# The gate's column sums spread over four due times, and later

## The chip, the cores and the metric

One core of one Trainium2 chip runs the kernel. The metric is the device time of one execution in microseconds (us). Three runs of the kernel before took 1739.5, 1739.6 and 1740.47 us; the median is 1739.6. One more execution was taken with the hardware profiler: 1735.66 us, of which the instructions span 1733.9 us.

## The reference

All data are float32, with 256 tokens and a width of 4096.

```
mod = SiLU(c) @ w_ada + b_ada              # -> shift, scale, gate (4096 each)
h   = RMSNorm(x) * (1 + scale) + shift
P   = h @ w_in                             # 4096 -> 14336 columns, in 7 groups of 2048
y_A = B * conv3(C * xa) * SiLU(z_A)        # causal depthwise conv over tokens
y_B = SiLU(LN(conv31(v * sigmoid(g)))) * SiLU(z_B)
x   = x + gate * ([y_A, y_B] @ w_out)      # 4096 -> 4096
out = RMSNorm(x) * final_g
```

The vector `gate` is needed only at the end, when the tiles of the output projection are finished.

## The kernel before, in words

**Matrix products.** Each f32 weight tile is loaded by SyncE's DMA queue (SP), in pieces of 256 rows by 512 columns (512 KB; a few of half that). ScalarE (ACT) rounds a piece to its high part (`w_h`, L217), VectorE (DVE) subtracts to get the low part (`w_l`, L218), and TensorE (PE) makes three products, high by high, high by low and low by high (L244 to L246). A slice of 128 rows takes 6 matmuls of 512 columns. The kernel counts its progress in these slices: `now` is the number of slices done, and is called the position here. A weight piece is mostly two slices, called a step. Positions 0 to 896 are the input projection, 896 to 1024 the first half of the output projection (tiles `pa0` to `pa7`, from the half y_A), 1024 to 1152 its second half (`pb0` to `pb7`, from y_B). Pieces are numbered in order: `w480` belongs to position 930, and `w519` to 1008.

**Buffers.** There are 4 buffers for raw pieces, 3 each for `w_h` and `w_l`, so a new piece can be rounded only when PE has ended with the piece three steps earlier. Pieces are asked for two steps ahead (`next_w`). Transposes and small reductions on PE go to a pool of two PSUM banks (`misc`), of which a new tile takes one that the program has already released.

**The modulation.** Columns of `shift`, `scale` and `gate` come from products of rows of w_ada with a broadcast SiLU(c) on DVE: one instruction (L271) for half of each of 128 columns, from a loaded row piece of 1 MB. These are called sums. There are 128 for shift and scale, and 64 for the gate (`gate0_0` to `gate31_1`), which fill the columns of `gateT`.

**Order of the work.** Everything is issued by a program written out in order. At each step `run_due` first issues what stands in `queue` with a due time at or before `now`. Then it takes from `filler`, the list of sums: a sum is issued when it is due, or ahead of that when a running estimate of DVE's and the DMA's load leaves room. The due times of the sums are interpolated along a hull of the points by which so many must be done (`need`). For all 64 gate sums one such point stands at position 1004. Four positions later `gate_store` transposes `gateT` on PE (L300), ACT copies the result four positions after that (L303) and writes it to `gate_d` in DRAM (L304). From there `load_resid` (L725 to L729) loads broadcast rows of `final_g` and of the gate, 1024 columns for two output tiles at a time, and `x` for each output tile, at positions 1026, 1042 and so on.

**Beside the products.** From about position 750 the 31-tap convolution of half B runs: ACT makes scaled copies (`pr`, L500), DVE adds them to `cv` (L503) or makes a tap by itself (L496). It goes on to position 970. Then the layer norm follows (`norm_B`, positions 972 to 1010), and at 1011 to 1025 the eight steps of `gate_B`: PE transposes 256 columns of SiLU(z_B) into a `misc` bank (`psZ0_0` to `psZ3_1`, L581), DVE multiplies `cv` by them (L584, called gated here), and both are split into `yT`. In the second half of the output projection DVE has three instructions per finished tile (L693, L696, L703).

The choice of what to take from the list of sums is this line:

```
due, mb, cost, f = filler[0]
if due > now and (max(vec, t - SLACK) + cost > t + UNIT * KD or max(load, t - SLACK) + mb / RATE > t + UNIT):
    break
```

Of the kernel before, what the change touches and what calls it, by code (L numbers as in the profile page):

```python
# [13 lines left out]
F32 = mybir.dt.float32  # L14
# [4 lines left out]
P = 128  # L19
D = 4096  # L20
S = 256
NS = S // P
KT = D // P
CT = 512
NE = 7 * 2048 // CT
NDT = D // CT
# [4 lines left out]
BLOCKS = (2, 4, 4, 4, 6, 6, 6)  # L31
# [3 lines left out]
KD = 2  # L35
# [6 lines left out]
UNIT = 1.363  # L42
FIRST = 29.0
RATE = 0.375
# [4 lines left out]
SLACK = 3.0  # L49
# [59 lines left out]
def decoder_block(ctx: ExitStack, tc: tile.TileContext, x, c, w_mod, w_gate, w_in, w_out, xt, pk, final_g, out):  # L109
    nc = tc.nc  # L110
# [11 lines left out]
    dram = ctx.enter_context(tc.tile_pool(name="dram", bufs=1, space=bass.MemoryType.DRAM))  # L122
# [3 lines left out]
    def bigt(name, shape=(P, 2, 512), dtype=F32):  # L126
        return big.tile(list(shape), dtype, tag="a", name=name)

    def misc(name, shape=(P, 512)):
        return pms.tile(list(shape), F32, tag="m", name=name)  # L130

    def pst(name):
        return pmm.tile([P, NS, CT], F32, tag="ps", name=name)
# [3 lines left out]
    ident = const.tile([P, P], F32, name="ident")  # L137
# [32 lines left out]
    end_in = sum(n for _, _, n in plan)  # L170
    start_last = sum(k1 - k0 for b, _, k0, k1 in SEGS if b < len(BLOCKS) - 1)
    conv_end = end_in + CONV_END
    plan += [(w_out[dt], k0 + k, KD) for k0 in (0, KT // 2) for dt in range(NDT) for k in range(0, KT // 2, KD)]
    loaded = []
    step = 0
    now = 0
    queue = []
    filler = []
    vec = load = 0.0

    def put(t, f, cost=0.0):
        queue.append((t, cost, f))
        queue.sort(key=lambda e: e[0])
# [5 lines left out]
    def run_due():  # L189

        nonlocal vec, load
        t = FIRST + UNIT * now
        while queue and queue[0][0] <= now:
            _, cost, f = queue.pop(0)
            vec = max(vec, t - SLACK) + cost
            f()
        while filler:
            due, mb, cost, f = filler[0]
            if due > now and (max(vec, t - SLACK) + cost > t + UNIT * KD or max(load, t - SLACK) + mb / RATE > t + UNIT):
                break  # L200
            filler.pop(0)
            vec = max(vec, t - SLACK) + cost
            load = max(load, t - SLACK) + mb / RATE
            f()
# [53 lines left out]
    gateT = const.tile([P, KT], F32, name="gateT")  # L258
# [4 lines left out]
    def ada_steps(name, srcs, bias, dst):  # L263

        at = next(part_no) % 4
        pt = pts[:, at:at + 1]

        def piece(q):
            raw = rows.tile([P, ROW], F32, tag="r", name=f"{name}_{q}")
            nc.sync.dma_start(raw, srcs[q])  # L270
            nc.vector.tensor_tensor_reduce(out=raw, in0=raw, in1=cB[:, q * ROW:(q + 1) * ROW], scale=1.0, scalar=pt if q else bias, op0=ALU.mult, op1=ALU.add, accum_out=dst if q else pt)  # L271

        return [lambda q=q: piece(q) for q in range(D // ROW)]

    def mod_steps(k):

        def scale(f):
            f()
            nc.vector.scalar_tensor_tensor(out=gscT[:, k:k + 1], in0=modT[:, 32 + k:33 + k], scalar=1.0, in1=pks[:, O_G + k:O_G + k + 1], op0=ALU.add, op1=ALU.mult)

        work = []
        for t in (1, 0):
            col = 32 * t + k
            work += ada_steps(f"mod{k}_{t}", w_mod[k, t], pks[:, O_BADA + col:O_BADA + col + 1], modT[:, col:col + 1])
        work[1] = lambda f=work[1]: scale(f)
        return work

    gate_d = dram.tile([D], F32, name="gate_d")
    gate = {}

    def gate_steps():
        return [f for k in range(KT) for f in ada_steps(f"gate{k}", w_gate[k], pks[:, O_BGATE + k:O_BGATE + k + 1], gateT[:, k:k + 1])]

    def gate_store():

        ps = misc("gate_ps", (P, P))
        row = bigt("gate_row", (P, P))

        def turn():
            nc.tensor.transpose(ps[:KT], gateT, ident)  # L300

        def store():
            nc.scalar.copy(row[:KT], ps[:KT])  # L303
            nc.scalar.dma_start(gate_d.rearrange("(k p) -> k p", p=P), row[:KT])  # L304

        turn()
        put(now + 2 * KD, store)
# [35 lines left out]
    for q in range(4):  # L343
        for s in range(NS):
            t = bigt(f"xn{q}_{s}", (P, 1024))
# [14 lines left out]
    for q in range(4):  # L360
        ps = pst(f"cps{q}")
# [7 lines left out]
    v, y, t = (tiny[:, i] for i in range(3))  # L369
# [12 lines left out]
    ps = misc("rstd_ps", (P, S))  # L382
# [12 lines left out]
    vec = load = FIRST - SLACK  # L395


    work = [f for k in range(1, KT) for f in mod_steps(k)]
    gates_due = end_in + KT // 2 * NDT - 20
    need = [(FIRST_USE[k] - H_DUE, len(work) * k // (KT - 1)) for k in range(1, KT)]  # L400
    work += gate_steps()
    need.append((gates_due, len(work)))
    hull = [(-3.0, 0)]
    while hull[-1][1] < len(work):
        t0, n0 = hull[-1]
        hull.append(max((p for p in need if p[1] > n0), key=lambda p: ((p[1] - n0) / max(p[0] - t0, 0.1), p[0])))
    for n, f in enumerate(work):
        filler.append((float(np.interp(n + 1, [d for _, d in hull], [t for t, _ in hull])), ADA_LOAD, ADA_SUM, f))
    put(gates_due + 4, gate_store)
    for ks in [[1]] + [[k, k + 1] for k in range(KD, KT, KD)]:  # L410
        for (f, cost), lead in zip(h_steps(ks), H_LEAD):
            put(FIRST_USE[ks[0]] - lead, f, cost)
# [180 lines left out]
    def seed(n):  # L593


        _, e, k0, _ = SEGS[n]
        ps = pst(f"ps{k0}_{e}")
        if k0:
            nc.scalar.copy(ps, acc[e])  # L599
        return ps  # L600
# [30 lines left out]
    ps = seed(0)  # L631
    for n, (b, e, k0, k1) in enumerate(SEGS):
        steps = _steps(k0, k1)
        for j, (k, m) in enumerate(steps):
            parts = begin_step()
            if j == max(len(steps) - 2, 0) and n + 1 < len(SEGS):
                ps_next = seed(n + 1)
            run_due()
            products(ps, act_h, parts, k, m, k == 0, k + m == k1, seeded=k0 > 0)
            advance()  # L640
        pending.append(lambda e=e, k1=k1, ps=ps: take(e, k1, ps))
        ps = ps_next
# [4 lines left out]
    for i in range(4):  # L647
        for h in range(2):
            t = end_in + NORM_AT + NORM_STEP * (19.5 + 2 * i + h)
# [20 lines left out]
    for dt in range(NDT):  # L670
        ps = pst(f"pa{dt}")
        for k in range(0, KT // 2, KD):
            parts = begin_step()
            if dt == NDT - 1 and k == KD * 4:
                ps_next = seed_b(0)
            run_due()
            products(ps, yT, parts, k, KD, k == 0, k + KD == KT // 2)
            advance()
        pending.append(lambda dt=dt, ps=ps: take_a(dt, ps))
# [7 lines left out]
    def finish_tile(dt, ps):  # L687

        o, xr = res[dt], resid[dt]
        g, fg = half(gate, dt), half(fgb, dt)  # L690

        def gated():
            nc.vector.tensor_tensor(out=o, in0=ps, in1=g, op=ALU.mult)  # L693

        def residual():
            nc.vector.tensor_tensor(out=o, in0=o, in1=xr, op=ALU.add)  # L696

        def squares():
            for s in range(NS):
                nc.scalar.activation(out=xr[:, s], in_=o[:, s], func=AF.Square, accum_out=sums[:, s, dt:dt + 1])  # L700

        def weighted():
            nc.vector.tensor_tensor(out=o, in0=o, in1=fg, op=ALU.mult)  # L703

        def ahead():
            table(AF.Sqrt)
            nc.vector.tensor_tensor(out=o, in0=o, in1=g, op=ALU.mult)
            nc.vector.tensor_tensor(out=o, in0=o, in1=xr, op=ALU.add)

        def last(s):  # L710
            t = scratch[:, s]
            nc.vector.tensor_tensor(out=t, in0=ps[s], in1=g[:, s], op=ALU.mult)
            nc.vector.tensor_tensor(out=o[:, s], in0=o[:, s], in1=t, op=ALU.add)
            nc.scalar.activation(out=t, in_=o[:, s], func=AF.Square, accum_out=sums[:, s, dt:dt + 1])
            nc.vector.tensor_tensor(out=o[:, s], in0=o[:, s], in1=fg[:, s], op=ALU.mult)

        if dt == NDT - 1:
            scratch = bigt(f"t{dt}")
            return [ahead] + [lambda s=s: last(s) for s in range(NS)]
        return [gated, residual, squares, weighted]  # L720

    def load_resid(dt):
        if dt % 2 == 0:
            t = fgb[dt // 2] = bigt(f"fg{dt // 2}", (P, 1024))
            nc.sync.dma_start(t, final_g[dt * CT:dt * CT + 1024].partition_broadcast(P))  # L725
            t = gate[dt // 2] = bigt(f"gate{dt // 2}", (P, 1024))
            nc.sync.dma_start(t, gate_d[dt * CT:dt * CT + 1024].partition_broadcast(P))
        xr = resid[dt] = bigt(f"xr{dt}")
        nc.sync.dma_start(xr, xv[:, :, dt * CT:(dt + 1) * CT])  # L729

# [8 lines left out]
    ps = ps_next  # L739
    for dt in range(NDT - 1):  # L740
# [8 lines left out]
        ps = ps_next  # L749
# [4 lines left out]
    for k in range(KT // 2, KT, KD):  # L754
        held[k] = begin_step()
        run_due()
        if k == KT // 2 + 4 * KD:
            work = finish_tile(NDT - 1, pss)
# [6 lines left out]
    for s in range(NS):  # L765
# [4 lines left out]
        v, y, t = (const.tile([P, 1], F32, name=f"o_{n}{s}") for n in "vyt")  # L770
# [47 lines left out]
```

## Time and profile before

| quantity | value |
|---|---|
| median of three runs | 1739.6 us |
| the profiled execution, whole | 1735.66 us |
| its span | 1733.9 us |
| PE busy | 1635.9 us, 94% |
| DVE busy | 1398.1 us, 81% |
| ACT busy | 1171.9 us, 68% |
| moved by DMA | 526.02 MB, mean 303 GB/s |

The profiled execution is 1.8 us longer than its span, and 3.9 us shorter than the median of the runs. Busy shares are averages over stages that have different limits: the stages have to be read one by one. In rows of a timeline a start and a duration are given; DVE overlaps the end of one instruction with the start of the next, so what an instruction costs DVE is better read from one start to the next.

### The profile page before, as it was taken

Reading aid. Unit: us, or ns where it says so; the run is one execution under the profiler, and the core shown is the slowest. Engines: PE = TensorE matmul, PEld = TensorE weight load, DVE = VectorE, ACT = ScalarE, POOL = GpSimd, SP = SyncE. Lnnn points to the kernel's source line nnn. Section 1 sums busy time; section 2 is a strip of 40 time slices with the busy share of each in tenths; the row PEclk is TensorE's granted clock in tenths of the full one; section 3 lists DMA queues with packets and bytes.
Section 4 is the critical chain, followed back from the end, with each engine's and each line's share of the span. In section 5 each row is a group of like instructions: output and inputs, shape, how many; then the busy total and the mean of one; then the engine's idle time right before and its main releaser. Section 6 shows DMA issues by size and latency. Waiting matters only on the chain.

```text
span 1733.9 us, 20044 instructions
## 1 busy us (share of the span) xinstructions
PE 1635.9 (94%) x7069; PEld 1321.2 (76%) x7069; DVE 1398.1 (81%) x1409; ACT 1171.9 (68%) x1525; POOL 1.0 (0%) x8
## 2 busy tenths in 40 slices
PE   6999999999999999999999999989988988899997
PEld 3668878888788788887888887777766766778885
DVE  6888877778777877778777778899999999875666
ACT  5787667666677666666656666999977775564444
POOL 0000000000000000000000000000000000000000
PEclk9999999999999999999999999999999999999999
DMA  9998999999999999999999999665666778667775
GB/s 363 373 380 334 370 336 336 331 346 357 342 349 348 358 336 344 348 353 361 338 349 342 349 359 336 205 188 165 194 232 222 286 258 292 240 195 248 242 240 190
DMA packets 122284, 526.02 MB, mean 303 GB/s; under 512 B 13476, under 2 KB 13764, under 8 KB 97608
## 3 DMA queue, kind: packets, MB, share of 16 engines
q1 hardware_dynamic: 121992, 524.36, 83.7%
q8 instruction: 56, 0.92, 0.2%
q10 hardware_dynamic: 192, 0.39, 0.1%
q14 instruction: 44, 0.36, 0.1%
HBM read 520.48 MB, written 4.21 MB: 303 GB/s over the span
## 4 chain that ended last, share of the span: by engine, by line
PE 62%; DVE 19%; issue 8%; ACT 5%; DMA 5%; SPq 0%; DVEq 0%; ACTq 0%
PE ps L246 17%; PE ps L244 17%; PE ps L245 17%; DVE w_l L218 7%; DVE cv L503 4%; DMA w_r<-in_w_in 4%; PE pb L245 3%; PE pb L244 3%; PE pb L246 3%; ACT w_h L217 2%; DVE gate L271 2%; DVE cv L496 2%; DMA mod<-in_w_mod 1%; DVE mod L271 1%; ACT acc L615 1%
## 5 line engine op out<-in xcount | busy, mean ns | idle before, releaser
L218 DVE TENSOR_TENSOR w_l<-w_r,w_h 128x1024 fp32r<-128x1024 f32 (+1 forms) x591 | 704.9, 1196 | 302.6 <-ACT w_h L217 301.9
L217 ACT CAST w_h<-w_r 128x1024 fp32r<-128x1024 f32 (+1 forms) x591 | 609.4, 1032 | 499.8 <-PE ps L246 325.6
L245 PE MATMUL ps<-w_l,hT 128*128 128x512 f32 x1792 | 703.9, 393 | 24.0 <-DVE w_l L218 23.8
L244 PE MATMUL ps<-w_h,hT 128*128 128x512 f32 x1792 | 705.6, 394 | 15.2 <-ACT hT L250 7.9
L246 PE MATMUL ps<-w_h,hT 128*128 128x512 f32 x1792 | 702.5, 392 | 9.5 <-DVE hT L253 9.4
L245 PEld LDWEIGHTS ps<-w_l,hT 128*128 128x128 f32 x1792 | 338.6, 189 | 102.6 <-DVE w_l L218 33.4
L244 PEld LDWEIGHTS ps<-w_h,hT 128*128 128x128 f32 x1792 | 338.4, 189 | 92.5 <-ACT hT L250 8.6
L246 PEld LDWEIGHTS ps<-w_h,hT 128*128 128x128 f32 x1792 | 338.4, 189 | 83.8 <-DVE hT L253 13.5
L615 ACT ACTIVATE acc<-ps 128x1024 f32<-128x1024 f32 x178 | 181.4, 1019 | 0.0
L599 ACT COPY ps<-acc 128x1024 f32<-128x1024 f32 x162 | 164.1, 1013 | 0.0
L500 ACT ACTIVATE pr<-uT,pks 128x254 f32<-128x254 f32 (+23 forms) x384 | 159.3, 496 | 0.0
L271 DVE CUSTOM_DVE_ANT_0 mod<-mod,cB,pks 128x2048 f32<-128x2048 f32 x64 | 150.2, 2346 | 2.7 <-DMA mod<-in_w_mod 2.7
L271 DVE CUSTOM_DVE_ANT_0 mod<-mod,cB,pts 128x2048 f32<-128x2048 f32 x64 | 150.2, 2347 | 2.6 <-DMA mod<-in_w_mod 2.6
L245 PE MATMUL pa<-w_l,yT 128*128 128x512 f32 x256 | 103.1, 403 | 14.2 <-DVE w_l L218 14.2
L503 DVE TENSOR_TENSOR cv<-cv,pr 128x1020 f32<-128x1020 f32 (+11 forms) x96 | 111.3, 1159 | 0.9
L244 PE MATMUL pa<-w_h,yT 128*128 128x512 f32 x256 | 102.6, 401 | 0.0
L246 PE MATMUL pa<-w_h,yT 128*128 128x512 f32 x256 | 101.1, 395 | 0.0
L244 PE MATMUL pb<-w_h,yT 128*128 128x512 f32 x256 | 99.8, 390 | 0.0
L246 PE MATMUL pb<-w_h,yT 128*128 128x512 f32 x256 | 99.6, 389 | 0.0
L245 PE MATMUL pb<-w_l,yT 128*128 128x512 f32 x256 | 99.6, 389 | 0.0
L271 DVE CUSTOM_DVE_ANT_0 gate<-gate,cB,pts 128x2048 f32<-128x2048 f32 x32 | 75.1, 2347 | 0.0
L271 DVE CUSTOM_DVE_ANT_0 gate<-gate,cB,pks 128x2048 f32<-128x2048 f32 x32 | 75.1, 2346 | 0.0
(112 smaller groups left out, 689.4 us busy)
## 6 DMA issues: line engine op xcount, KB each, us to landing
w_r<-in_w_in SPq DMA_DIRECT2D x433, 512.0 KB, 5.3
mod<-in_w_mod SPq DMA_DIRECT2D x128, 1024.0 KB, 7.2
gate<-in_w_gate SPq DMA_DIRECT2D x64, 1024.0 KB, 6.5
w_r<-in_w_out SPq DMA_DIRECT2D x128, 512.0 KB, 4.4
w_r<-in_w_in SPq DMA_DIRECT2D x30, 256.0 KB, 5.7
xn<-in_x SPq DMA_DIRECT2D x8, 512.0 KB, 5.8
xr<-in_x SPq DMA_DIRECT2D x8, 512.0 KB, 6.9
out<-o SPq DMA_DIRECT2D x16, 256.0 KB, 2.4
```

The costliest lines, as they stand in the source:

```text
L217: nc.scalar.copy(hi[:, part], raw[:, part])
L218: nc.vector.tensor_tensor(out=lo[:, part], in0=raw[:, part], in1=hi[:, part].bitcast(F32), op=ALU.subtract)
L244: nc.tensor.matmul(out, ah, hi[:, i], start=f, stop=False, skip_group_check=seeded)
L245: nc.tensor.matmul(out, ah, lo[:, i], start=False, stop=False, skip_group_check=seeded)
L246: nc.tensor.matmul(out, al, hi[:, i], start=False, stop=l, skip_group_check=seeded)
L271: nc.vector.tensor_tensor_reduce(out=raw, in0=raw, in1=cB[:, q * ROW:(q + 1) * ROW], scale=1.0, scalar=pt if q else bias, op0=ALU.mult, op ...
L496: nc.vector.scalar_tensor_tensor(out=o[:, j, sh:], in0=u[:, j, :S - sh], scalar=cbw[:, 4 * i + j, TAPS - 1 - sh:TAPS - sh], in1=o[:, j, sh ...
L500: nc.scalar.activation(out=pr[:, j, sh:], in_=u[:, j, :S - sh], func=AF.Copy, scale=cbw[:, 4 * i + j, TAPS - 1 - sh:TAPS - sh])
L503: nc.vector.tensor_tensor(out=o[:, :, sh:], in0=o[:, :, sh:], in1=pr[:, :, sh:], op=ALU.add)
L599: nc.scalar.copy(ps, acc[e])
L615: nc.scalar.activation(out=acc[e], in_=ps, func=func)
```

## The change

Three things are changed.

1. Past the position `last_vg` = 722 + 8 x 6 = 770 a sum is issued only when it is due, never ahead.
2. The one point of `need` for the gate (all sums by 1004) becomes four: a quarter of them by 1008, by 1040, by 1072 and by 1104. By the hull, sums that are left at 770 are spread evenly, one per some 6.4 positions, to 1104.
3. `gate_store` becomes four: each transposes 8 columns of `gateT` six positions after its point (1014, 1046, 1078, 1110), copies and writes them four positions later into a DRAM tile of its own (`gate_d0` to `gate_d3`), and `load_resid` reads that tile. The positions of the loads stay.

```diff
+    last_vg = start_last + 8 * BLOCKS[-1]
...
-            if due > now and (max(vec, t - SLACK) + cost > t + UNIT * KD or max(load, t - SLACK) + mb / RATE > t + UNIT):
+            if due > now and (now > last_vg or max(vec, t - SLACK) + cost > t + UNIT * KD or max(load, t - SLACK) + mb / RATE > t + UNIT):
...
-    gate_d = dram.tile([D], F32, name="gate_d")
+    gate_d = [dram.tile([1024], F32, name=f"gate_d{q}") for q in range(4)]
...
-    def gate_store():
+    def gate_store(q):
...
-            nc.tensor.transpose(ps[:KT], gateT, ident)
+            nc.tensor.transpose(ps[:8], gateT[:, 8 * q:8 * q + 8], ident)
...
-    gates_due = end_in + KT // 2 * NDT - 20
...
-    work += gate_steps()
-    need.append((gates_due, len(work)))
+    gates = gate_steps()
+    for q in range(4):
+        gates_due = end_in + KT // 2 * (NDT + 2 * q) - 16
+        need.append((gates_due, len(work) + len(gates) * (q + 1) // 4))
+        put(gates_due + 6, lambda q=q: gate_store(q))
+    work += gates
...
-    put(gates_due + 4, gate_store)
...
-            nc.sync.dma_start(t, gate_d[dt * CT:dt * CT + 1024].partition_broadcast(P))
+            nc.sync.dma_start(t, gate_d[dt // 2].partition_broadcast(P))
```

Where the sums go is shown by the order of instructions. Up to position 770 both programs have issued 35 of the 64. Before, the other 29 follow the low parts at positions 776, 796, 860 and then one per some 5.5 positions to 1008. After, they follow those at 930, 936, 942 and so on to 1108.

DVE in the convolution, position 880 (`w455` to `w458` are low parts, `cv2` the convolution, `yfA3` the short one), before:

```order
L218 TENSOR_TENSOR w455_l_9984<-w455_r_9981,w455_h_9983 128x1024
L503 TENSOR_TENSOR cv2_8518<-cv2_8518,pr2_8_9960 128x4x248
L218 TENSOR_TENSOR w456_l_10013<-w456_r_10010,w456_h_10012 128x1024
L496 SCALAR_TENSOR_TENSOR cv2_8518<-uT2_8474,pks_60,cv2_8518 128x246 x4
L503 TENSOR_TENSOR cv2_8518<-cv2_8518,pr2_9_9987 128x4x247
L443 SCALAR_TENSOR_TENSOR yfA3_0_10017<-psA12_9993,pks_60,yfA3_0_10017 128x255
L443 SCALAR_TENSOR_TENSOR yfA3_0_10017<-psA12_9993,pks_60,yfA3_0_10017 128x254
L444 TENSOR_TENSOR yfA3_0_10017<-yfA3_0_10017,psA12_9993 128x256
L271 ISA gate20_1_10027,gateT_102<-gate20_1_10027,cB_104,pts_103 128x2048
L271 ISA gateT_102 128x1
L218 TENSOR_TENSOR w457_l_10045<-w457_r_10042,w457_h_10044 128x1024
```

And the same place on DVE in the changed program:

```order
L219 TENSOR_TENSOR w455_l_9969<-w455_r_9966,w455_h_9968 128x1024
L506 TENSOR_TENSOR cv2_8521<-cv2_8521,pr2_8_9948 128x4x248
L219 TENSOR_TENSOR w456_l_9998<-w456_r_9995,w456_h_9997 128x1024
L499 SCALAR_TENSOR_TENSOR cv2_8521<-uT2_8477,pks_60,cv2_8521 128x246 x4
L506 TENSOR_TENSOR cv2_8521<-cv2_8521,pr2_9_9972 128x4x247
L446 SCALAR_TENSOR_TENSOR yfA3_0_10002<-psA12_9978,pks_60,yfA3_0_10002 128x255
L446 SCALAR_TENSOR_TENSOR yfA3_0_10002<-psA12_9978,pks_60,yfA3_0_10002 128x254
L447 TENSOR_TENSOR yfA3_0_10002<-yfA3_0_10002,psA12_9978 128x256
L219 TENSOR_TENSOR w457_l_10027<-w457_r_10024,w457_h_10026 128x1024
```

The sum is gone from between two low parts, and all else stands as it stood. The same holds for every sum of before between positions 776 and 928.

PE at position 1014, in the eight steps of `gate_B` (`psZ0_1` is the second of them, `pa7` the last tile of the first half), before:

```order
L246 MATMUL pa7_11645<-w521_h_11648,yT2_9383 128x512
L581 MATMUL psZ0_1_11733<-ident_90,acc24_695 128x128 x4
L244 MATMUL pa7_11645<-w522_h_11676,yT3_9509 128x512
L245 MATMUL pa7_11645<-w522_l_11677,yT3_9509 128x512
L246 MATMUL pa7_11645<-w522_h_11676,yT3_9509 128x512
```

And PE there in the changed program:

```order
L247 MATMUL pa7_11600<-w521_h_11603,yT2_9380 128x512
L584 MATMUL psZ0_1_11686<-ident_90,acc24_698 128x128 x4
L301 MATMUL gate_ps0_11692<-ident_90,gateT_102 8x128
L245 MATMUL pa7_11600<-w522_h_11631,yT3_9506 128x512
L246 MATMUL pa7_11600<-w522_l_11632,yT3_9506 128x512
```

The transpose of the gate stood at position 1008, ahead of `psZ0_0`; its first quarter now stands right behind `psZ0_1`, and takes a `misc` bank in the middle of the eight. In the built program `gate_ps0` lies in one of the two banks until its copy at position 1018, and `psZ0_1`, `psZ1_0` and `psZ1_1` all lie in the other; before, these alternate.

DVE at position 1058, in the second half of the output projection (`o1` is a tile being finished), before:

```order
L218 TENSOR_TENSOR w544_l_12176<-w544_r_12173,w544_h_12175 128x1024
L218 TENSOR_TENSOR w545_l_12194<-w545_r_12191,w545_h_12193 128x1024
L218 TENSOR_TENSOR w546_l_12212<-w546_r_12209,w546_h_12211 128x1024
L693 TENSOR_TENSOR o1_10700<-pb1_12006,gate0_11907 128x1024
L218 TENSOR_TENSOR w547_l_12237<-w547_r_12234,w547_h_12236 128x1024
L696 TENSOR_TENSOR o1_10700<-o1_10700,xr1_12063 128x1024
L218 TENSOR_TENSOR w548_l_12256<-w548_r_12253,w548_h_12255 128x1024
```

And DVE there in the changed program:

```order
L219 TENSOR_TENSOR w544_l_12157<-w544_r_12154,w544_h_12156 128x1024
L272 ISA gate27_1_12160,gateT_102<-gate27_1_12160,cB_104,pts_103 128x2048
L272 ISA gateT_102 128x1
L219 TENSOR_TENSOR w545_l_12178<-w545_r_12175,w545_h_12177 128x1024
L219 TENSOR_TENSOR w546_l_12196<-w546_r_12193,w546_h_12195 128x1024
L696 TENSOR_TENSOR o1_10661<-pb1_11976,gate0_11871 128x1024
L219 TENSOR_TENSOR w547_l_12221<-w547_r_12218,w547_h_12220 128x1024
L699 TENSOR_TENSOR o1_10661<-o1_10661,xr1_12036 128x1024
L272 ISA gate28_0_12225,pts_103<-gate28_0_12225,cB_104,pks_60 128x2048
L272 ISA pts_103 128x1
L219 TENSOR_TENSOR w548_l_12243<-w548_r_12240,w548_h_12242 128x1024
```

Sums now stand among the low parts and the finishing instructions of the second half, 14 of them behind positions 1026 to 1108, where there were none.

## Rows read from the trace of the kernel before

**Rows 1.** The page: its span, and each engine's busy time.

```profile
span 1733.9 us, 20044 instructions
PE 1635.9 (94%) x7069; PEld 1321.2 (76%) x7069; DVE 1398.1 (81%) x1409; ACT 1171.9 (68%) x1525; POOL 1.0 (0%) x8
```

**Rows 2.** Windows: start:end, length, busy PE, PEld, DVE, ACT, POOL, clock, DMA, GB/s.

```profile
1140.00:1257.30 117.30, 108.55 (x487) 86.91 (x487) 112.46 (x140) 112.25 (x204) 0.00 (x0) 1.00 0.60 185
1257.30:1385.40 128.10, 109.30 (x448) 86.01 (x446) 127.29 (x151) 99.31 (x183) 0.00 (x0) 0.93 0.70 249
1385.40:1453.20 67.80, 59.67 (x249) 46.88 (x248) 67.59 (x71) 52.14 (x96) 0.00 (x0) 0.97 0.76 272
1453.20:1549.40 96.20, 84.21 (x367) 65.99 (x366) 78.08 (x81) 50.55 (x64) 0.00 (x0) 0.98 0.69 236
1549.40:1710.00 160.60, 160.60 (x711) 133.06 (x712) 102.07 (x89) 81.15 (x100) 0.00 (x0) 1.00 0.73 233
```

**Rows 3.** Windows of the gate's sums alone: DVE busy, clock, DMA, GB/s.

```profile
1257.30:1385.40 128.10, 30.50 (x13) 0.93 0.70 249
1385.40:1459.40 74.00, 18.77 (x8) 0.98 0.77 277
```

**Rows 4.** Waits of PE from 1257.3 to 1385.4: us in total, times, longest.

```profile
PE ps L245 <- DVE w_l L218: 14.5, 6, 3.5
PE pa L245 <- DVE w_l L218: 4.3, 4, 1.8
```

**Rows 5.** Timeline of DVE: one sum, and the start of what follows.

```profile
1314.24 2.35 DVE L271 CUSTOM_DVE_ANT_0 gate<-gate,cB,pks 128x2048 f32<-128x2048 f32 x1
1316.51 1.22 DVE L218 TENSOR_TENSOR w_l<-w_r,w_h 128x1024 fp32r<-128x1024 f32 x1
```

**Rows 6.** Lines of the window 1257.3 to 1385.4, ACT: its casts.

```profile
L217 ACT CAST w_h<-w_r 128x1024 fp32r<-128x1024 f32 x36 | 37.8, 1050 | 17.7 <-PE pa L246 10.9 <-PE ps L246 5.2 <-ACT pr L500 0.7
```

**Rows 7.** Waits of PE and PEld around the gate's transpose, 1453 to 1546.

```profile
PE gate_ps L300 <- DVE gateT L271: 3.0, 1, 3.0
PE psZ L581 <- ACT gate_row L303: 0.3, 1, 0.3
```

**Rows 8.** Timeline of PE: the third and fourth psZ.

```profile
1532.10 0.63 PE L581 MATMUL psZ<-ident,acc 128*128 128x128 f32 x4
1535.56 0.63 PE L581 MATMUL psZ<-ident,acc 128*128 128x128 f32 x4
```

**Rows 9.** Timeline of DVE and ACT in the same steps.

```profile
1533.59 1.23 DVE L218 TENSOR_TENSOR w_l<-w_r,w_h 128x1024 fp32r<-128x1024 f32 x1 [1.64 <-ACT w_h L217]
1534.73 0.68 DVE L584 TENSOR_TENSOR cv<-cv,psZ 128x512 f32<-128x512 f32 x1
1532.51 1.04 ACT L217 CAST w_h<-w_r 128x1024 fp32r<-128x1024 f32 x1
```

**Rows 10.** Timeline of ACT in the second half: two casts in sequence.

```profile
1588.21 1.06 ACT L217 CAST w_h<-w_r 128x1024 fp32r<-128x1024 f32 x1 [0.75 <-PE pb L246]
1590.93 1.06 ACT L217 CAST w_h<-w_r 128x1024 fp32r<-128x1024 f32 x1 [1.66 <-PE pb L246]
```

**Rows 11.** Window of the short convolution's transposes (tile psA): PE, PEld, DVE, ACT.

```profile
1257.30:1385.40 128.10, 3.83 (x24) 3.20 (x24) 9.66 (x21) 3.22 (x7) 0.93 0.70 249
```

**Rows 12.** DMA, 43 to 217: rate in 40 slices; its whole; sums' and weights' landing.

```profile
GB/s 256 325 347 352 397 359 428 419 426 420 423 428 423 402 346 388 408 333 340 307 211 391 267 351 310 344 404 381 397 288 347 370 353 368 365 394 398 358 383 369
DMA packets 14617, 63.40 MB, mean 364 GB/s; under 512 B 1620, under 2 KB 1620, under 8 KB 10815
w_r<-in_w_in SPq DMA_DIRECT2D x52, 512.0 KB, 6.0
```

**Rows 13.** The gate's row in DRAM: us from issue to landing.

```profile
DMA to landing us min/median/max: 3.8/3.8/3.8
```

**Rows 14.** Timeline of SP: loads of an even tile in the second half.

```profile
1586.02 0.42 SPq L727 DMA_DIRECT2D gate<-gate_d  x1
1587.83 19.41 SPq L212 DMA_DIRECT2D w_r<-in_w_out  x8
```

More of the change, by code (lines that the diff above doesn't have):

```diff
@@ L292, in gate_steps @@
         return [f for k in range(KT) for f in ada_steps(f"gate{k}", w_gate[k], pks[:, O_BGATE + k:O_BGATE + k + 1], gateT[:, k:k + 1])]
-    def gate_store():
-        ps = misc("gate_ps", (P, P))
-        row = bigt("gate_row", (P, P))
+    def gate_store(q):
+        ps = misc(f"gate_ps{q}", (P, P))
+        row = bigt(f"gate_row{q}", (P, P))
         def turn():
-            nc.tensor.transpose(ps[:KT], gateT, ident)
+            nc.tensor.transpose(ps[:8], gateT[:, 8 * q:8 * q + 8], ident)
         def store():
-            nc.scalar.copy(row[:KT], ps[:KT])
-            nc.scalar.dma_start(gate_d.rearrange("(k p) -> k p", p=P), row[:KT])
+            nc.scalar.copy(row[:8], ps[:8])
+            nc.scalar.dma_start(gate_d[q].rearrange("(k p) -> k p", p=P), row[:8])
         turn()
```

## The prediction

> **What bounds the kernel now.** I read the page's shares first, then the span by windows, then the waits inside each window. PE is busy 94% of the span [rows 1], so the loss is local. From position 1024 on PE is the bound: it is busy 160.60 of 160.60 us while DVE has 102.07 [rows 2]. A step of two positions takes 1590.93 - 1588.21 = 2.72 us there, 1.36 per position [rows 10].
>
> In the convolution it is otherwise. From 1257.3 to 1385.4 DVE is busy 127.29 of 128.10 us [rows 2]. All that PE waits for there is a low part from DVE, 14.5 + 4.3 us [rows 4], and its mean granted clock of 0.93 says that part of the stretch ran at 1.2 and not 2.4 GHz. DVE is the bound, and 13 gate sums with 30.50 us stand in that stretch [rows 3]. From 1140 to 1257.3 DVE and ACT are nearly full together (112.46 and 112.25 of 117.30), with almost no sum; this stretch shows how close to a full engine the kernel gets when several are full: 112.46 / 117.30 = 96% [rows 2].
>
> **What the 13 sums are worth: -24 us.** By the order, the sums of before that follow positions 860 to 928 are these 13, and the changed program has none between 770 and 930. A sum costs DVE 1316.51 - 1314.24 = 2.27 us from its start to the next one's [rows 5], so DVE is relieved of 13 x 2.27 = 29.5 us and would need 128.1 - 29.5 = 98.6. The other two come close. PE: ACT's 36 casts there [rows 6] mean 35 to 36 steps; 35 x 2.72 = 95.2 us, and 24 transposes in six groups of four [rows 11], each 1535.56 - 1532.10 - 2.72 = 0.74 us [rows 8, 10], 4.4 more: 99.6. ACT: 99.31 busy [rows 2]. So nothing can make the stretch shorter than 99.6 us, a gain of 28.5. With three engines that full I apply the 96% of the stretch ahead: 99.6 / 0.96 = 103.8, a gain of 24.3; I take 24. The low end is a stretch only 90% full (110.7 us), a gain of 17; I keep 14 as the end, since ACT's copies and DVE's additions of one tap follow each other. Two sums at positions 776 and 796 go too. They stand where ACT is the fuller engine, so I count 0 (at most 2 x 2.27 = 4.5). From 930 to 975 there are 8 sums before [rows 3] and 8 after: 0.
>
> **The norm and the steps of gate_B: +4 us.** From 1453 to 1549 PE waits on DVE again and again. From 980 to 1008 there are six sums before and five after. One less in that chain is worth 0 to 2.3 us; I take -1. The transpose of the gate makes PE wait 3.0 us at position 1008, for the last sum, and `psZ0_1` 0.3 for its copy [rows 7]. Both go, since the first quarter's columns were finished long before position 770: -3.3 (at least 0, if the next low part is late instead).
>
> A new wait comes. `gate_ps0` holds one of the two `misc` banks from 1014 to 1018, and three psZ tiles follow each other in the other. `psZ1_0` may now start only when DVE has read `psZ0_1`. Before, that read began at 1534.73 and took 0.68 us, to 1535.41, and `psZ1_0` had started at 1532.10 [rows 8, 9]: 1535.41 - 1532.10 = 3.3 us of waiting that the second bank had hidden. It can't come sooner, as DVE's low part ahead of it (1533.59) needs ACT's cast (1532.51), which needs the buffer of the step that PE has just ended. For `psZ1_1` the same chain is cast 1.04, low part 1534.73 - 1533.59 = 1.14 from start to start [rows 9], read 0.68, some 3 us after PE ends `w523`; a sum (2.27) stands on DVE in that step as well, beside PE's step of 2.72. Behind PE all weights and transposes queue, and from here it has no slack to make good. I take 3.3 + 3.2 = +6.5; the ends are 0 (DVE ahead of PE by a step more) and 8.8 (the sum wholly in the way). Later quarters have the banks for themselves. Two sums at 1026 and 1032 are new on DVE between psZ reads, where it idled 1.64 us in a step [rows 9]; 2.27 exceeds this by 0.6 each: +1 (0 to 2.5). In all -1 - 3.3 + 6.5 + 1 = +3.2.
>
> **The second half of the output projection: +1.5 us.** 14 sums stand behind positions 1026 to 1108, one per 6.4 positions, that is per 8.7 us. DVE has 102.07 / 160.60 = 64% without them [rows 2], and 2.27 / 8.7 = 26% is added: 90%. Whether PE waits is a matter of order. A low part must be there by the end of three steps from when its buffer comes free, less the step then running: PE frees the buffer, ACT casts (1.06 us, [rows 10]), DVE has until two steps later, 5.44 us. So 5.44 - 1.06 - 1.23 = 3.15 us of lateness are free. One sum of 2.27 fits; at position 1058 a finishing instruction (as long as a low part, 1.2) and a sum come together, 3.5 us, less the 1.5 that DVE has over in the step. It fits, and the next two steps make it good. DVE: 0, at most 14 x 2.27 = 31.8 if nothing hid.
>
> The DMA queue: from 1026 to 1108, 82 positions or 111.5 us, it moves 41 pieces of w_out (21.5 MB), 14 row pieces (14.7), five of x (2.6) and three pairs for `final_g` and gate (3.1), 41.9 MB or 376 GB/s; before it was 233 [rows 2]. From 43 to 217 us, the densest comparable stretch, the mean was 364 GB/s, and there eight slices of 4.35 us in a row had 402 to 428 [rows 12]. So the rate is to be had, though not with ease: at 364 the pieces would take 115.1 us, 3.6 more. I take +1.5, ends 0 and 6. By the Trainium skill (DMA: Bandwidth & Descriptors, Specifications) the limit of HBM for one core is about 358 GB/s; an estimate by that figure is 41.9 MB in 117 us, 5.5 more, and the forecast would be 4 us later. The trace does not bear it out as a limit, since 428 stands in its slices [rows 12].
>
> The quarters' loads: a row lands 3.8 us after its issue [rows 13]. SP reaches the load of the gate at its position while PE is some 6 to 8 positions behind, about where the copy now stands, and so may wait 2 to 4 us each time. The first weight piece behind the load left 1587.83 - 1586.02 = 1.8 us later anyway, waiting for a buffer [rows 14], and a piece that lands in 6.0 us [rows 12] has three steps until it is used. 0, at most 4 x 2 = 8. Three more transposes, copies and writes: under 0.3 us each on PE, within the 1.5.
>
> **The sum.** -24 + 3.2 + 1.5 = -19.3 us against the profiled execution, 1735.66 - 19.3 = 1716.4. That execution was 3.9 us under the median of the runs, so for the median 1739.6 - 19.3 = 1720.3; I say 1720.
>
> **The rivals.**
> *The full relief* (chance 0.13): the stretch falls to its floor (-28.5) and the bank costs nothing (-1 - 3.3 + 1): -31.8 + 1.5, so 1709. For it: PE's waits there are on DVE alone [rows 4]. Against it: three engines at 99 us each.
> *ACT takes over* (0.13): the scaled copies come late as soon as DVE is not, as at 1140 to 1257 where ACT had 112.25 of 117.30 [rows 2]. The gain is 10 in place of 24: 1734. Against it: in the stretch ACT waited for PE 16.1 us [rows 6], so it is ahead.
> *The transfers come late* (0.13): 364 GB/s or less behind position 1026, and SP's waits for the quarters add to it: +3.6 to +8 in place of 1.5, about 1726.
> *Slower* (0.08): the late sums are not hidden. Place: DVE between two low parts from 1026 to 1108. Price: 14 x 2.27 = 31.8 us on an engine that has no other slack, against the 20.8 saved up to the start of that half: 1720.3 - 1.5 + 31.8 = 1751. It decides from a cost of 20.8 / 14 = 1.5 us per sum. For it: low parts stand right behind the sums in the order. Against it: 58.5 us of idle DVE in that half (160.60 - 102.07, [rows 2]) and a lateness of 3.15 us that is free.
> *That the sums don't move* has no chance: the order shows each of them in its new place.
>
> **How the numbers follow.** The forecast has 0.53, and 1720. A change of 0.2% (3.5 us) is about what a measurement of this kernel can tell from none. Faster by more than that: 0.53 + 0.13 + 0.13, and 0.09 of the case of ACT: 0.88. Within 0.2%: 0.05, of the case of ACT and of partly hidden sums. Slower: 0.07. The forecast's own range by its ends is 1710 to 1731; with the cases of ACT and of the full relief it is 1707 to 1735.
>
> **What would show it.** In the convolution, from the sum's last at 770 to 930: the same 70 positions in about 104 us, DVE and ACT both over 93% busy, the clock nearer to 1, PE's waits on `w_l` down from 18.8 us to under 5. At the psZ steps: two PE waits of about 3 us on L587's read, no wait of 3 us at the gate's transpose. In the second half: PE full at 2.72 us per step, DVE near 90% from 1026 to 1108, and DMA about 370 GB/s. It is wrong if PE waits there for low parts by more than a few microseconds, or if the stretch of the convolution is still over 114 us long.

## The result, and the profile after

In the comparison the changed kernel took 1724.35 us (median of 4 runs, 1722.4 to 1726.97) against 1739.55 us before: a ratio of 0.9915, with a 95% interval of 0.9898 to 0.9933. That is 15.2 us less (some 12 to 18 by the interval). 19.3 less had been forecast, as 1720 us. The two profiled executions, 1735.66 and 1723.02 us, differ by 12.6 us only: the one before lies 3.9 us under the median of its runs, the one after 1.3 us under its own. What follows accounts for these 12.6 us.

The two traces were laid side by side by position: the time at which ACT's cast of the piece that belongs to a position starts, after less before. A falling number is time won, a rising one time lost. ACT casts a piece some three steps before PE takes it up, so the second row gives the same for the start of PE's first matmul of the position (each trace holds all 6912 matmuls with weights, six per position).

| position | 864 | 896 | 928 | 976 | 992 | 1008 | 1024 | 1040 | 1072 | 1104 | 1136 |
|---|---|---|---|---|---|---|---|---|---|---|---|
| cast, after - before, us | -1.8 | -12.0 | -23.8 | -28.2 | -28.2 | -25.0 | -14.3 | -13.2 | -12.5 | -12.9 | -12.7 |
| PE, after - before, us | -1.8 | -16.7 | -23.8 | -28.2 | -28.2 | -29.3 | -14.3 | -13.2 | -13.0 | -12.9 | -12.7 |

By position 976 the change had won 28.2 us, and between 976 and 1040 it gave 15.0 of them back. The second half of the output projection, with its 14 new sums, gave back 0.5. The stages of the changed kernel answer to [rows 2] and have the same columns. Each of the first three windows lies between the same two matmuls of PE as its counterpart there (448, 249 and 367 of them); the fourth is a part of the second half.

```profile
1255.54:1361.59 106.05, 101.71 (x448) 82.22 (x447) 101.54 (x126) 98.57 (x183) 0.00 (x0) 0.98 0.62 193
1361.59:1424.93 63.34, 58.16 (x249) 45.62 (x248) 63.13 (x69) 51.73 (x96) 0.00 (x0) 1.00 0.77 268
1424.93:1535.03 110.10, 91.97 (x367) 72.73 (x365) 82.81 (x84) 50.37 (x63) 0.00 (x0) 0.89 0.69 238
1540.00:1648.00 108.00, 108.00 (x479) 89.21 (x478) 91.33 (x82) 52.46 (x65) 0.00 (x0) 1.00 0.94 352
```

The convolution's stretch went from 128.1 to 106.1 us, with PE, DVE and ACT each 93 to 96% busy; PE's waits for low parts in it, 18.8 us in [rows 4], are these:

```profile
PE ps L246 <- DVE w_l L219: 4.3, 4, 2.0
```

The third window is the loss. It is longer than the one before (110.1 against 96.2 us), and its mean granted clock fell from 0.98 to 0.89. PE's waits in it, to be read against [rows 7]:

```profile
PE psZ L584 <- DVE cv L587: 7.5, 3, 3.1
PE gate_ps L301 <- DVE cv L587: 3.2, 1, 3.2
```

The timeline of PE has them in order, from the second psZ on; the psZ that did not wait are left out behind the fourth (start, duration, and in brackets the idle time ahead and its releaser):

```profile
1499.41 0.60 PE L584 MATMUL psZ<-ident,acc 128*128 128x128 f32 x4
1503.21 0.37 PE L301 MATMUL gate_ps<-ident,gateT 128*8 128x128 f32 x1 [3.20 <-DVE cv L587]
1510.86 1.08 PE L584 MATMUL psZ<-ident,acc 128*128 128x128 f32 x4 [3.13 <-DVE cv L587]
1520.09 1.07 PE L584 MATMUL psZ<-ident,acc 128*128 128x128 f32 x4 [3.13 <-DVE cv L587]
1536.21 0.63 PE L584 MATMUL psZ<-ident,acc 128*128 128x128 f32 x4 [1.25 <-DVE cv L587]
```

Three waits of 3.1 to 3.2 us stand in a row, where two had been forecast: the first quarter's transpose itself waits too, since its bank had held `psZ0_0` and DVE had not yet read that. What follows each wait is slow. Four transposes take 1.08 us in place of 0.63, and windows between the waits show the granted clock:

```profile
1505.00:1511.00 6.00, 2.87 (x10) 1.96 (x9) 2.11 (x3) 2.21 (x3) 0.00 (x0) 0.78 0.66 260
1511.00:1520.00 9.00, 5.96 (x16) 4.38 (x16) 4.47 (x6) 1.44 (x3) 0.00 (x0) 0.68 0.16 58
1520.00:1525.00 5.00, 4.92 (x18) 4.08 (x18) 0.54 (x1) 0.75 (x2) 0.00 (x0) 0.66 0.65 214
```

Means of 0.66 to 0.78 say that PE ran much of its time there at 1.2 and not 2.4 GHz, after idling for 3 us out of every 6 to 9.

### The profile page after: what moved, and what is told of

Read it like the earlier page. It is cut to its first block, busy times and chain, and to the rows that moved or that the text cites. A ratio compares the mean times of both kernels' runs of the same rounds, so it can differ in the third digit from the quotient of the medians.

```text
span 1721.2 us, 20069 instructions
## 1 busy us (share of the span) xinstructions
PE 1635.4 (95%) x7072; PEld 1323.4 (77%) x7072; DVE 1397.7 (81%) x1409; ACT 1169.3 (68%) x1528; POOL 1.0 (0%) x8
## 4 chain that ended last, share of the span: by engine, by line
PE 66%; DVE 15%; issue 7%; ACT 6%; DMA 5%; SPq 0%; DVEq 0%; ACTq 0%
PE ps L247 17%; PE ps L246 17%; PE ps L245 17%; DVE w_l L219 5%; DMA w_r<-in_w_in 3%; PE pb L246 3%; PE pb L247 3%; PE pb L245 3%; ACT w_h L218 3%; DVE cv L506 2%; DMA mod<-in_w_mod 2%; PE pa L246 2%; PE pa L247 1%; PE pa L245 1%; DVE cv L499 1%
## 5 line engine op out<-in xcount | busy, mean ns | idle before, releaser
L245 PE MATMUL ps<-w_h,hT 128*128 128x512 f32 x1792 | 704.2, 393 | 15.2 <-ACT hT L251 7.7
L246 PE MATMUL ps<-w_l,hT 128*128 128x512 f32 x1792 | 702.4, 392 | 12.7 <-DVE w_l L219 12.5
L247 PEld LDWEIGHTS ps<-w_h,hT 128*128 128x128 f32 x1792 | 337.8, 188 | 82.1 <-DVE hT L254 11.8
L602 ACT COPY ps<-acc 128x1024 f32<-128x1024 f32 x162 | 164.0, 1012 | 0.0
L245 PE MATMUL pa<-w_h,yT 128*128 128x512 f32 x256 | 104.6, 409 | 0.0
L247 PE MATMUL pa<-w_h,yT 128*128 128x512 f32 x256 | 102.9, 402 | 0.0
```

What stands on the lines that cost most here:

```text
L245: nc.tensor.matmul(out, ah, hi[:, i], start=f, stop=False, skip_group_check=seeded)
L246: nc.tensor.matmul(out, ah, lo[:, i], start=False, stop=False, skip_group_check=seeded)
L247: nc.tensor.matmul(out, al, hi[:, i], start=False, stop=l, skip_group_check=seeded)
```

## The experiments

Theory B is that the bank that the first quarter holds from 1014 to 1018 costs the 13 to 15 us of the steps of `gate_B`, by waits and by the clock behind them. Rival S puts the loss on the two new sums at 1012 and 1020, rival N on the norm's chain, which would take back what was won whatever PE does.

**The first quarter stored early.**

```diff
-        put(gates_due + 6, lambda q=q: gate_store(q))
+        put(gates_due + 6 if q else 1000, lambda q=q: gate_store(q))
```

> The changed kernel, with the first quarter's transpose and copy moved from positions 1014 and 1018 to 1000 and 1004, so that the two misc banks alternate again in the eight steps of gate_B. Theory B (the bank): three reads of psZ that PE waits for (3.2, 3.1, 3.1 us) and the lower clock that follows them cost 14 us of the stretch from the first psZ to the last (40.0 us after, 24.4 before). Expected 1711 us (1708 to 1715), psZ stretch about 25 us, no PE wait on the reads over 1.5 us. Rival S (the sums at 1012 and 1020 hold up DVE in that stretch): 1721 to 1725, the waits stay. Rival N (the norm's chain takes the gain back whatever PE does): 1719 to 1724, with PE waiting longer for the means instead.

Measured: 1711.67 us, ratio 0.9835 (0.9822 to 0.9849). In the table's terms 1008 to 1040 goes from +11.8 to -1.6. Of the waits this is left:

```profile
PE psZ L584 <- DVE cv L587: 3.0, 3, 1.2
```

Theory B holds, in size too. S and N fall as the main cause; these 3.0 us are what is left for the sums.

**The bank alone, in the kernel before.**

```diff
-    put(gates_due + 4, gate_store)
+    put(gates_due + 10, gate_store)
```

> The kernel before, with its one gate transpose moved from position 1008 to 1014 and the copy from 1012 to 1018; all sums stay. Theory B: the bank alone makes the same three waits, 9.5 us, and some 5 us of lower clock, less the 3.3 us that PE waited at 1008: 1748 to 1752 us. Rival S (late sums are the cause): 1736 to 1740, since no sum stands between 1012 and 1026 here. Rival N: 1739 to 1741.

Measured: 1749.25 us, ratio 1.005 (1.0036 to 1.0064), 8.5 slower than before. No sum was moved. By position the trace was 3.8 us later than before already at 600, ahead of anything that was edited; from there on the difference arises from 1008 to 1024 (+10.5; 0.2 from 864 to 1008, 0.0 from 1024 to 1136). The three waits are there:

```profile
PE psZ L581 <- DVE cv L584: 6.3, 2, 3.1
PE gate_ps L300 <- DVE cv L584: 2.7, 1, 2.7
```

**The four parts without the new rule, and the rule without the parts.** The first is the run with the early store less `now > last_vg or`; the second is the kernel before with it.

> As the run with the first store early, but without the new rule past position 770 (sums may again go ahead when the estimate has room). By its order three sums go ahead to 788, 806 and before 942, where ACT is the full engine. If the four due times carry the gain: within 3 us of the run with the rule, 1709 to 1715. If the rule carries it: 1730 or more.

> The kernel before with the new rule alone (one due time at 1004, one store at 1008). By its order it only moves two sums, from 776 and 796 to 848 and 854. If the due times carry the gain: 1738 to 1744, the same as before or up to 4 us slower. If the rule carries it: 1725 to 1730.

Measured: 1709.92 us, ratio 0.9828 (0.9813 to 0.9842), and 1742.95 us, ratio 1.0015 (1.0005 to 1.0026). The later due times carry the gain. The rule adds nothing to them, and alone it costs about 2 us: by position the two sums that it moves to 848 and 854 cost 2.8 + 1.7 = 4.5 us there, which is 2 x 2.27, the price of a sum in [rows 5], and their old places give back less than 1.

**PE kept busy in two of the three waits**, to part the clock from the waits.

```diff
...
+            if i == 1:
+                y = yT[KT // 2 - 1][:, 0]
+                for _ in range(24):
+                    nc.tensor.matmul(spare[0][:, P:P + S], y[:, :P], y, start=True, stop=True)
             ps = st["ps"] = misc(f"psZ{i}_{h}", (P, 2, S))
```

> The changed kernel, with 24 matmuls of 256 columns (2.7 us; their products go into unused columns of the gate's bank and are read by nobody) ahead of the third and the fourth psZ, where PE otherwise waits 3.1 us each. Theory: of the 14 us that the steps of gate_B cost over the run with the first store early, 9.5 are waits and some 4.5 are matmuls at the lower clock after them, 1.5 us per wait; kept busy in two of three, PE keeps its clock: 1720 to 1722 us, and the steps behind these two psZ take 2.7 to 3.0 us and not 4.2. Rival (the steps behind are long because a low part is late, not for the clock): 1724 to 1726.

Measured: 1720.9 us, ratio 0.9905 (0.9889 to 0.9921). From 1008 to 1024 the table would read +6.5 in place of +10.7. These are the granted clock of the stretch in which it had been 0.66 to 0.78, the two filled places, and the second psZ behind them, with 0.26 us of idle time left ahead of it (as ahead of the first):

```profile
1503.00:1526.00 23.00, 21.46 (x117) 18.35 (x118) 10.42 (x13) 7.48 (x10) 0.00 (x0) 0.93 0.60 202
1508.42 3.03 PE L585 MATMUL gate_ps<-yT 128*128 128x256 f32 x24
1514.94 3.03 PE L585 MATMUL gate_ps<-yT 128*128 128x256 f32 x24
1518.23 0.63 PE L589 MATMUL psZ<-ident,acc 128*128 128x128 f32 x4 [0.26 <-DVE cv L592]
```

The psZ still start when DVE lets them; only what PE does meanwhile is other, and 4.2 us come back in the trace: that share of the loss was the clock. The medians differ by 3.5, but the intervals of the two ratios overlap, so this rests on the place in the trace.

**The late sums squeezed.** The run with the four parts and without the new rule, with sums due after 1004 put at `1028 + (at - 1004) * 0.76`.

> As the run with four parts and no new rule, with the sums that were due from 1008 to 1104 squeezed into 1032 to 1104, so that none stands in the eight steps of gate_B: 16 in 72 positions, 98 us. DVE then needs 0.64 x 98 + 16 x 2.27 = 99 us there. Theory (a sum is hidden as long as DVE is not full, and the sums in gate_B cost the 3.0 us of waits that its PE rows show): 3 less, 1 to 2 more, 1707 to 1710 us. Rival (a sum right ahead of a low part delays PE well before DVE is full): 1713 to 1725.

Measured: 1709.13 us, ratio 0.9835 (0.9819 to 0.985), not to be told from the 1709.92 without the squeeze. In gate_B PE's wait for psZ fell from 3.0 to 0.6 us. In the stretch behind it DVE was busy 86.24 of 98 us, the DMA queue moved 382 GB/s, and the waits of PE and of its weight loads (PEld) for low parts were these:

```profile
PE psZ L587 <- DVE cv L590: 0.6, 1, 0.6
1538.00:1636.00 98.00, 96.47 (x422) 78.34 (x421) 86.24 (x77) 44.60 (x56) 0.00 (x0) 1.00 0.99 382
PE pb L246 <- DVE w_l L219: 1.5, 3, 0.8
PEld pb L246 <- DVE w_l L219: 3.0, 4, 1.1
```

Four steps of PE are longer than 2.72 us by it, 2.8 us in all. So a sum per 4.5 positions is no longer hidden whole, and it is not DVE that ran out (16 x 2.27 + 0.64 x 98 = 99 us was too much: DVE had 86). In the two longest of the four the low part was late because a weight was: ACT's cast waited for its transfer (5.53 and 5.83 us), DVE for the cast, PE for the low part. The first of the two:

```profile
1570.54 1.05 ACT L218 CAST w_h<-w_r 128x1024 fp32r<-128x1024 f32 x1 [5.53 <-DMA w_r<-in_w_out]
1571.62 1.23 DVE L219 TENSOR_TENSOR w_l<-w_r,w_h 128x1024 fp32r<-128x1024 f32 x1 [3.54 <-ACT w_h L218]
1572.91 0.50 PE L246 MATMUL pb<-w_l,yT 128*128 128x512 f32 x1 [0.60 <-DVE w_l L219]
```

**Sums ahead, by the estimate of the DMA's rate.** In the run with the early store `RATE` becomes 0.4 past position 600, and in a second one past 250; a third gives the kernel before the same rate past 250, and nothing else.

```diff
-            if due > now and (... mb / RATE > t + UNIT):
+            if due > now and (... mb / (0.4 if now > 250 else RATE) > t + UNIT):
...
-            load = max(load, t - SLACK) + mb / RATE
+            load = max(load, t - SLACK) + mb / (0.4 if now > 250 else RATE)
```

> As the run with the first store early, but past position 600 the estimate of the DMA's rate that lets sums go ahead is 0.4 and not 0.375 MB per us. By its order sums go at one per 4 positions from 600 to 770 in place of one per 5, and 21 in place of 29 are left; the eight between 930 and 972 are gone. The queue must then move 0.54 MB per position, 397 GB/s. If the rate of 402 to 428 GB/s seen in slices is to be had: no loss before 770, and 5 to 7 us won at 930 to 976: 1704 to 1707 us. If the 364 GB/s of the densest stretch is the limit: 170 positions x 0.12 us = 20 us lost, 1720 to 1726.

> As the run with the rate of 0.4 past position 600, but with that rate past 250. By its order 59 of the 64 gate sums are issued by 764 and the last five between 1084 and 1108, so none is left in the convolution's second half, the norm and gate_B. If the queue keeps up with 0.54 MB per position over 500 positions as it did over 170 (PE full, 386 GB/s), the sums gone from 974 to 1080 are worth 3 to 7 us more: 1698 to 1703. If it falls behind over the longer stretch: 1706 to 1720, with ACT waiting for weights before 770.

> The kernel before (one due time, one store at 1008) with the rate of 0.4 past position 250 and nothing of the change. By its order two sums are left at 776 and 796 and two at 982 and 990. If what counts is only that the sums stand clear of the stretch where DVE is full: within 4 us of the run with four parts and that rate, 1698 to 1706. If the later due times have a worth of their own: 1712 or more.

Measured: 1705.3 us, ratio 0.9806 (0.979 to 0.9823); 1690.39 us, ratio 0.9724 (0.9711 to 0.9737); and 1693.19 us, ratio 0.9741 (0.9726 to 0.9756). The queue keeps up, and PE has no more idle time for it (windows of the first and of the second run):

```profile
870.00:1050.00 180.00, 180.00 (x796) 149.17 (x795) 152.64 (x133) 110.97 (x113) 0.00 (x0) 1.00 1.00 386
330.00:1050.00 720.00, 714.96 (x3148) 590.04 (x3147) 614.24 (x556) 460.44 (x479) 0.00 (x0) 1.00 1.00 382
```

The second run is 8 us below the low end of what I expected. The place is the norm, and to a small part gate_B: from 976 to 1024 its difference to the kernel before grows by 12.3 us (-32.2 to -44.5), against 0.8 in the first run (-30.7 to -31.5), which has eight sums there. Without sums in DVE's queue PE's waits for the two means, in the first run

```profile
PE mu_ps L528 <- DVE mu_t L523: 4.3, 1, 4.3
PE var_ps L528 <- DVE var_t L523: 3.7, 1, 3.7
```

are in the second

```profile
PE var_ps L528 <- DVE var_t L523: 0.6, 1, 0.6
PE mu_ps L528 <- DVE mu_t L523: 0.4, 1, 0.4
```

And the kernel before, with that rate alone, comes within 3 us of the second run (under the 1698 to 1706 that I had put on it). That the due times are four and late is not what counts; that the sums stand clear of the convolution and of the norm is.

## Why the prediction was right, and where not

**The 13 sums: -24 forecast.** From 864 to 928 the trace shows -22.0, and from 928 to 976 another 4.4, for which I had counted 0. One of the 13 belongs to these 4.4: it follows the low part of position 928, so that nine sums of before stand behind 928 to 974 and eight of after. At 2.27 us for it the 13 are worth 24.3 in all. The other 2.1 are not traced to an instruction; the clock there is 1.00 in place of 0.97. The stretch came out at 106.05 us where 103.8 had been forecast, with the three engines at 93 to 96%. The two sums at 776 and 796, counted as 0, gave 1.8.

**The norm and gate_B: +3.2 forecast (the heading of the term says +4), +15.0 measured.** This step failed, in its size; the mechanism, one bank held while three psZ share the other, was right and is shown by the runs that move the store alone, in both directions. By PE's starts the four parts of the term are these: the norm (976 to 1000) +3.2 for a forecast of -1; the old transpose's wait (1000 to 1008) -4.3 for -3.3; the bank (1008 to 1020) +15.1 for +6.5; the later psZ (1020 to 1026) +1.0 for +1.

Two things were missing from the +6.5. The transpose itself waits for a bank: 3.2 us, so the waits come to 9.5. And the matmuls after a wait of 3 us ran at the lower clock, which is most of the rest: 4.2 us of it came back with PE kept busy in two of three waits. I had reckoned each wait as time lost once.

In the norm the same happened once more. PE's waits for the two means were 4.3 and 2.4 us before and are 2.6 and 3.7 now, no more in sum. But behind the second one the granted clock, which had stayed at 1.00, was 0.59 for 7 us (before, then after):

```profile
1497.82 1.13 PE L525 MATMUL var_ps<-var_t,mean_w 128*128 128x256 f32 x4 [2.35 <-DVE var_t L520]
1497.80:1504.80 7.00, 6.98 (x31) 5.83 (x32) 4.94 (x5) 2.89 (x4) 0.00 (x0) 1.00 0.94 359
1470.12 2.08 PE L528 MATMUL var_ps<-var_t,mean_w 128*128 128x256 f32 x4 [3.71 <-DVE var_t L523]
1470.00:1477.00 7.00, 6.88 (x19) 5.49 (x20) 3.46 (x4) 0.31 (x1) 0.00 (x0) 0.59 0.83 308
```

One sum less in that stretch was thus worth nothing. No run takes the clock alone out of this place.

**The second half: +1.5 forecast, +0.5 measured.** PE is busy 108.00 of 108.00 us, DVE 85% (forecast 90%), DMA 352 GB/s (forecast 376). Every step of PE from 1028 to 1110 takes 2.72 us, as before, but for those with the transposes of the three later quarters, 0.16 us each, which are the whole +0.5. So that a sum fits in the free lateness of a low part is borne out at a sum per 6.4 positions. The limit of about 358 GB/s for one core of the Trainium skill (DMA: Bandwidth & Descriptors, Specifications), which I had set aside, is exceeded for 720 us on end at 382 GB/s here. The Trainium skill (HBM Reference, Specifications (TRN2)) says that a core that streams alone gets well above that share; the runs here, with one core, agree.

**The number.** That 1724.35 lies inside the range of 1710 to 1731 is in part luck. The term of the norm and gate_B, at 15.0, is above the sum of its own upper ends (0 + 0 + 8.8 + 2.5 = 11.3). The other terms together came out 5.2 us better than forecast, and the medians lie 2.6 us further apart than the two traces.

**The rivals.** None came. The nearest by its time, late transfers (1726), was nearer than the time shows: transfers did come late, but PE lost nothing by it. The quarters' loads held up SP, by 4.2 us at the first (1519.79 plus 0.38 to 1524.41, for a copy that was issued at 1520.78 only) and 9.1 us in all. From 1540 to 1648 six casts of ACT waited 12.5 us for weights, where none did in the same steps before; the longest stands behind the loads of the second quarter. The three steps until a piece is used took this up, and PE's steps stayed at 2.72 us:

```profile
1519.79 0.38 SPq L728 DMA_DIRECT2D fg<-in_final_g  x1
1524.41 0.33 SPq L730 DMA_DIRECT2D gate<-gate_d  x1
SPq L730 <- DMA gate_d<-gate_row: 9.1, 4, 4.2
ACT w_h L218 <- DMA w_r<-in_w_out: 12.5, 6, 4.1
1588.67 1.05 ACT L218 CAST w_h<-w_r 128x1024 fp32r<-128x1024 f32 x1 [4.05 <-DMA w_r<-in_w_out]
```

## What to carry to other kernels

Movable work is best placed by which engine is full in each stretch: here one sum cost 2.27 us where DVE was full, some 1.4 us in the norm and gate_B (12.3 - 0.8 = 11.5 us for eight sums), and nothing where PE was the bound, as long as the DMA queue kept up. When a small tile is moved into a place where a pool of two banks alternates, count every wait that the lost alternation makes, the tile's own among them, and add what PE loses at the lower clock after it. An estimate in a planner (here a DMA rate of 0.375) may hold more than a new rule: raising it to 0.4 was worth three times the change.

## What was not expected of the hardware

Waits of PE of some 3 us, three within 20 us, brought the granted clock to 0.66 to 0.78 between them, so that 10.7 us of waits (3.20 + 3.13 + 3.13 + 1.25) became some 16 (-29.3 to -13.2 by PE's starts, from 1008 to 1026). One DMA queue of 512 KB and 1 MB loads gave 382 GB/s over 720 us at a busy share of 1.00, with PE 99% busy.
